# Modulation columns begun from GpSimd's queue in place of the queue that carries the weights

## The chip, the cores and the metric

The kernel runs on one core of one Trainium2 chip. The metric is the device time of one execution in microseconds (us), from the first to the last thing the core does for the program.

## The reference, cut to what matters

Two transformer blocks run one after the other on one sequence of 256 tokens with a width of 2048, all in float32. The first block takes six modulation vectors (shift, scale and gate, twice) from a conditioning vector `c`. The second block has no modulation.

```python
c_act = jax.nn.silu(c)
mod = c_act @ w_ada[l] + b_ada[l]                      # w_ada is 2048 x 12288
sh1, sc1, gt1, sh2, sc2, gt2 = jnp.split(mod, 6, axis=-1)
h = modulate(rms_norm(x, g_mix[l]), sh1, sc1)          # h * (1 + scale) + shift
z = h @ w_in[l]                                        # 2048 x 11344
...                                                    # two attentions, gates, two output products
x = x + gt1[:, None, :] * (merged @ w_out[l])
h = modulate(rms_norm(x, g_ffn[l]), sh2, sc2)
...                                                    # gated feed-forward
x = x + gt2[:, None, :] * y
```

So `sh1` and `sc1` are needed before the first large product can begin, `gt1` after the attentions, and the other three later. The second block is a gated linear attention and another feed-forward.

## The kernel before

Activations lie with features on the 128 partitions and the 256 tokens along a row, so a product needs weight tiles of 128x128 (or, for values, 128x512) in SBUF. Every weight tile group goes through `weights` (L89 to L102): a DMA on SyncE's queue brings 128x1024 float32 (512 KB) into a tile `raw`, ScalarE rounds it to `hi` (L96), VectorE subtracts to get the rest `lo` (L97), and TensorE multiplies `hi` and `lo` with the split activations. There are four buffers each of `raw`, `hi` and `lo`. Nearly all the rest of the kernel is this stream: 916 such groups in 2.7 ms. "Group n" below is the n-th of these, counted from 0, told by the n-th L97.

The modulation is not done on TensorE. The transposed `w_ada` is 96 blocks of 128x2048 float32 (1 MB each), one for each of 6 vectors times 16 feature tiles. `mod_fetch` (L200 to L207) takes the next block from a list `modq` and starts its DMA into a tile `col`, of which there are two buffers; `mod_reduce` (L209 to L215) multiplies it on VectorE by the broadcast `c_act` and sums along the row (L212), which gives one column of one vector. A third column can be fetched only when the first has been reduced.

In `mixer` the first 32 columns are interleaved with the first product, tile by tile: feature tile k of the activations (`h_mod`: L298 and L301 on VectorE, L300 on ScalarE) needs columns 2k and 2k+1. The first product is done in parts, `batch(b, k0, k1)`, for three groups of outputs b and for the feature tiles 0 to 1, 2 to 6 and 7 to 15, so that not all 16 tiles are needed at once; it takes 96 weight groups, and its products are L134, L135 and L136. The other 64 columns are spread by a credit (`self.rate`) over the weight groups that follow; fetches and weights are marked as of high priority.

The order of the instructions on each engine, and on each DMA queue, is not written by hand: the framework's scheduler sets it when the program is built, from the code's order, the priorities and its own estimate of durations. Once built it is fixed, and each engine and queue works in that order, waiting where something is not ready. Before the change every DMA of the program, columns and weights alike, is issued by SyncE's queue (SP); GpSimd (POOL) does nothing but four small memory settings at the start.

Of the kernel before, what the change touches and what calls it, by code (L numbers as in the profile page):

```python
# [19 lines left out]
KD = D // P  # L20
# [12 lines left out]
class Core:  # L33
# [166 lines left out]
    def mod_fetch(self, offset=120):  # L200
        if not self.modq:
            return
        ci, j = self.modq.popleft()
        with self.tc.high_priority(offset=offset):
            col = self.wp.tile([P, D], F32, name="col", tag="col", bufs=2)
            self.nc.sync.dma_start(col, self.ap["w_ada"][ci * KD + j])
        self.colq.append((ci, j, col))  # L207

    def mod_reduce(self):  # L209
# [930 lines left out]
```

## Time and profile before

| | |
|---|---|
| median of 2 runs | 2692.26 us (2686.73 to 2697.78) |
| the profiled execution's own time | 2694.12 us |
| its span, first to last instruction | 2692.3 us |
| mean granted TensorE clock | 0.997 of 2.4 GHz |
| TensorE (PE) matmul busy | 2661.8 us, 99% |
| VectorE (DVE) busy | 1875.0 us, 70% |
| ScalarE (ACT) busy | 1304.5 us, 48% |
| DMA | 585.64 MB, mean 218 GB/s |

The busy share of PE is an upper bound for the work done, since matmuls are pipelined and their ends are modelled. Shares over the whole span hide that the first 700 us, in which the columns are fetched, are unlike the rest: there the DMA engines and VectorE are much busier than later.

### The profile page before, as it was taken

How to read it: one execution, taken by the hardware profiler on the slowest of the kernel's cores; microseconds unless marked ns; L12 is line 12 of the kernel's file. 1: busy time of each engine (PE TensorE's matmuls, PEld its weight loads, DVE VectorE, ACT ScalarE, POOL GpSimd, SP SyncE). 2: the span in 40 equal slices, each digit the busy share in tenths (PEclk: the TensorE clock that was granted, in tenths of full speed). 3: DMA queues.
4: the chain of work that ended last, by engine and by line, in shares of the span. 5: the costliest groups of instructions: out<-in, count | busy, mean ns of one | idle time of the engine just before them, and what ended most of it. 6: DMA issues, size and time to landing. Idle time of an engine off the chain costs nothing.

```text
span 2692.3 us, 41008 instructions
## 1 busy us (share of the span) xinstructions
PE 2661.8 (99%) x15996; PEld 2352.1 (87%) x15996; DVE 1875.0 (70%) x2725; ACT 1304.5 (48%) x1927; POOL 0.2 (0%) x4
## 2 busy tenths in 40 slices
PE   7999999999999999999999999999999999999999
PEld 6999977889988888888888888888888888888888
DVE  7998897978877666666555677477666666665444
ACT  5433344544555444444444565465544444444333
POOL 0000000000000000000000000000000000000000
PEclk9999999999999999999999999999999999999999
DMA  9989889888655555555666545545555555556664
GB/s 347 344 331 330 326 296 308 318 303 316 233 172 188 188 188 189 190 189 187 188 188 188 178 142 150 171 148 188 181 180 188 188 188 188 188 188 184 201 198 144
DMA packets 153853, 585.64 MB, mean 218 GB/s; under 512 B 17047, under 2 KB 21879, under 8 KB 141369
## 3 DMA queue, kind: packets, MB, share of 16 engines
q1 hardware_dynamic: 153658, 583.02, 63.9%
q8 instruction: 125, 2.05, 0.3%
q14 instruction: 70, 0.57, 0.1%
HBM read 579.22 MB, written 3.67 MB: 217 GB/s over the span
## 4 chain that ended last, share of the span: by engine, by line
PE 88%; DMA 5%; DVE 4%; issue 2%; ACT 1%; SPq 0%; DVEq 0%; ACTq 0%
PE acc L107 47%; PE acc L110 24%; DMA col<-in_w_ada 4%; PE acc L136 3%; PE acc L135 3%; PE acc L134 2%; DVE lo L97 2%; PE misc L134 1%; PE misc L135 1%; PE misc L136 1%; PE acc L174 1%; PE acc L175 1%; PE acc L176 1%; DVE col L212 1%; PE misc L878 1%
## 5 line engine op out<-in xcount | busy, mean ns | idle before, releaser
L107 PE MATMUL acc<-slot,hi 128*128 128x512 f32 x5520 | 1847.5, 395 | 3.0 <-ACT hi L96 2.5
L97 DVE TENSOR_TENSOR lo<-raw,hi 128x1024 fp32r<-128x1024 f32 (+1 forms) x916 | 1101.3, 1205 | 695.9 <-ACT hi L96 694.9
L96 ACT CAST hi<-raw 128x1024 fp32r<-128x1024 f32 (+1 forms) x916 | 946.5, 1034 | 1222.3 <-issue 525.9
L110 PE MATMUL acc<-slot,lo 128*128 128x256 f32 x5520 | 1326.4, 281 | 0.8 <-DVE lo L97 0.8
L110 PEld LDWEIGHTS acc<-slot,lo 128*128 128x128 f32 x5520 | 1039.5, 188 | 116.9 <-DVE lo L97 1.1
L107 PEld LDWEIGHTS acc<-slot,hi 128*128 128x128 f32 x5520 | 948.0, 188 | 127.6 <-ACT hi L96 2.8
L212 DVE CUSTOM_DVE_ANT_0 col<-col,big,vecs 128x2048 f32<-128x2048 f32 x96 | 225.4, 2348 | 44.3 <-DMA col<-in_w_ada 44.1
L134 PE MATMUL acc<-slot,hi 128*128 128x256 f32 x656 | 182.7, 284 | 8.8 <-ACT hi L96 4.6
L135 PE MATMUL acc<-slot,hi 128*128 128x256 f32 x656 | 183.2, 283 | 0.2 <-DVE slot L301 0.2
L136 PE MATMUL acc<-slot,lo 128*128 128x256 f32 x656 | 177.8, 285 | 1.4 <-DVE lo L97 1.1
L134 PEld LDWEIGHTS acc<-slot,hi 128*128 128x128 f32 x656 | 124.0, 190 | 10.3 <-ACT hi L96 5.8
L135 PEld LDWEIGHTS acc<-slot,hi 128*128 128x128 f32 x656 | 124.8, 190 | 0.5 <-DVE slot L301 0.5
L136 PEld LDWEIGHTS acc<-slot,lo 128*128 128x128 f32 x656 | 121.4, 191 | 3.1 <-DVE lo L97 3.1
L134 PE MATMUL misc<-slot,hi 128*128 128x256 f32 x384 | 107.6, 283 | 0.6 <-ACT hi L96 0.6
L135 PE MATMUL misc<-slot,hi 128*128 128x256 f32 x384 | 107.2, 281 | 0.0
L136 PE MATMUL misc<-slot,lo 128*128 128x256 f32 x384 | 105.3, 282 | 1.8 <-DVE lo L97 1.8
L174 PE MATMUL acc<-hi,slot 128*128 128x512 f32 x256 | 103.2, 403 | 0.0
L175 PE MATMUL acc<-lo,slot 128*128 128x512 f32 x256 | 101.2, 395 | 0.0
L176 PE MATMUL acc<-hi,slot 128*128 128x512 f32 x256 | 101.1, 395 | 0.0
L185 ACT COPY t<-acc 128x256 f32<-128x256 f32 x234 | 85.7, 366 | 0.7 <-PE acc L110 0.7
L186 DVE TENSOR_TENSOR t<-acc,t 128x256 f32<-128x256 f32 x188 | 78.5, 418 | 0.0
L134 PEld LDWEIGHTS misc<-slot,hi 128*128 128x128 f32 x384 | 72.6, 189 | 1.3 <-ACT hi L96 1.2
(222 smaller groups left out, 1619.3 us busy)
## 6 DMA issues: line engine op xcount, KB each, us to landing
raw<-in_w_gu SPq DMA_DIRECT2D x344, 512.0 KB, 3.6
col<-in_w_ada SPq DMA_DIRECT2D x96, 1024.0 KB, 7.6
raw<-in_w_in_k SPq DMA_DIRECT2D x96, 512.0 KB, 6.7
raw<-in_w_down SPq DMA_DIRECT2D x80, 512.0 KB, 4.3
raw<-in_w_dn SPq DMA_DIRECT2D x80, 512.0 KB, 4.5
raw<-in_gla_b SPq DMA_DIRECT2D x66, 512.0 KB, 3.6
raw<-in_w_in_b SPq DMA_DIRECT2D x50, 512.0 KB, 5.7
raw<-in_w_in_a SPq DMA_DIRECT2D x32, 512.0 KB, 5.8
```

The lines of the kernel that those rows point to most:

```text
L96: self.mark = nc.scalar.copy(hi[:, :n], raw[:, :n])
L97: nc.vector.tensor_sub(lo[:, :n], raw[:, :n], hi[:, :n])
L107: self.nc.tensor.matmul(acc, hi, x, start=start, stop=stop, skip_group_check=True)
L110: self.nc.tensor.matmul(acc[:, 1], lo, x[:, 0], start=False, stop=stop, skip_group_check=True)
L134: nc.tensor.matmul(out, hi, x[:, 0], start=first, stop=False, **mm)
L135: nc.tensor.matmul(out, hi, x[:, 1], start=False, stop=False, **mm)
L136: nc.tensor.matmul(out, lo, x[:, 0], start=False, stop=last, **mm)
L174: nc.tensor.matmul(o, hs[k][:, 0, tt], hi[:, w], start=(k == 0), stop=False)
L175: nc.tensor.matmul(o, hs[k][:, 0, tt], lo[:, w], start=False, stop=False)
L176: nc.tensor.matmul(o, hs[k][:, 1, tt], hi[:, w], start=False, stop=(k == KD - 1))
L185: nc.scalar.copy(t, acc[:, 1])
L212: self.nc.vector.tensor_tensor_reduce(out=col, in0=col, in1=self.c_act, scale=1.0, scalar=self.vec["b_ada"][:, n:n + 1], op0=ALU.mult, op1 ...
```

## The change

One call moves from SyncE's queue to GpSimd's.

```diff
@@ mod_fetch
         ci, j = self.modq.popleft()
         with self.tc.high_priority(offset=offset):
             col = self.wp.tile([P, D], F32, name="col", tag="col", bufs=2)
-            self.nc.sync.dma_start(col, self.ap["w_ada"][ci * KD + j])
+            self.nc.gpsimd.dma_start(col, self.ap["w_ada"][ci * KD + j])
         self.colq.append((ci, j, col))
```

Since the scheduler builds the order anew, the change also moves instructions on all engines up to group 214 or so. Three places follow. A name such as `slot_203` is a buffer of activations (tile 0 of the modulated input), `mod_78` holds the scale vector, `mod_77` the shift vector, and `t_201` is an intermediate of `h_mod`.

SyncE's queue at the start, before: after the input tiles and the vectors come two columns and then weights and columns in turn.

```order
L517 DMA slot_94<-in_x 128x512
L519 DMA vecs<-in_vecs 128x356
L206 DMA col<-in_w_ada 128x2048 x2
L93 DMA raw<-in_w_in_k 128x1024 x2
L206 DMA col<-in_w_ada 128x2048 x2
L93 DMA raw<-in_w_in_k 128x1024 x2
L206 DMA col<-in_w_ada 128x2048
L93 DMA raw<-in_w_in_k 128x1024
```

The same place after: weights follow at once, and no column is on this queue.

```order
L517 DMA slot_94<-in_x 128x512
L519 DMA vecs<-in_vecs 128x356
L93 DMA raw<-in_w_in_k 128x1024 x6
L334 DMA cst<-in_cst 128x512
```

GpSimd after: the 96 columns stand alone behind the four settings, of which this is the last.

```order
L1128 MEMSET const-uint8-127 128x1
L1135 UNCONDITIONAL_BRANCH
L206 DMA col<-in_w_ada 128x2048 x96
L1135 UNCONDITIONAL_BRANCH
L1135 ISA
```

The 96 column transfers have moved and wait only for a free `col` buffer there.

ScalarE at the start, before: the square root of the norm (L243) stands right behind the squares of the input (L523).

```order
L523 ACTIVATE slot_115<-slot_94 128x512
L243 ACT_TABLE_LOAD
L243 ACTIVATE slot_159<-misc,eps 128x256
L96 CAST hi<-raw 128x1024 x2
L300 ACTIVATE slot_203<-t_201,mod_77 128x256
```

The same place after.

```order
L523 ACTIVATE slot_115<-slot_94 128x512
L96 CAST hi<-raw 128x1024 x3
L243 ACT_TABLE_LOAD
L243 ACTIVATE slot_159<-misc,eps 128x256
L96 CAST hi<-raw 128x1024
L300 ACTIVATE slot_203<-t_201,mod_77 128x256
```

Three weight casts now stand ahead of the square root.

VectorE between the first and the second column's reduction and the low half of activation tile 0 (L301), before.

```order
L212 ISA col,mod_78<-col,big,vecs 128x2048
L212 ISA mod_78 128x1
L244 RECIPROCAL slot_159<-slot_159 128x256
L555 SCALAR_TENSOR_TENSOR mod_78<-mod_78,vecs 128x1
L212 ISA col,mod_77<-col,big,vecs 128x2048
L212 ISA mod_77 128x1
L97 TENSOR_TENSOR lo<-raw,hi 128x1024
L298 SCALAR_TENSOR_TENSOR t_201<-slot_87,mod_78,slot_159 128x256
L97 TENSOR_TENSOR lo<-raw,hi 128x1024
L301 SCALAR_TENSOR_TENSOR slot_203<-t_201,mod_77,slot_203 128x256
```

The same place after; the first column's reduction and two L97 stand ahead of these rows.

```order
L555 SCALAR_TENSOR_TENSOR mod_78<-mod_78,vecs 128x1
L212 ISA col,mod_77<-col,big,vecs 128x2048
L212 ISA mod_77 128x1
L97 TENSOR_TENSOR lo<-raw,hi 128x1024 x2
L244 RECIPROCAL slot_159<-slot_159 128x256
L212 ISA col,mod_78<-col,big,vecs 128x2048
L212 ISA mod_78 128x1
L298 SCALAR_TENSOR_TENSOR t_201<-slot_87,mod_78,slot_159 128x256
L555 SCALAR_TENSOR_TENSOR mod_78<-mod_78,vecs 128x1
L212 ISA col,mod_77<-col,big,vecs 128x2048
L212 ISA mod_77 128x1
L301 SCALAR_TENSOR_TENSOR slot_203<-t_201,mod_77,slot_203 128x256
```

Two more column reductions and two more L97 now stand ahead of the first finished activation tile.

Counted along VectorE's row order: ahead of group 56 there are 32 column reductions before and after the change; from there up to group 168 there are 45 before and 64 after; behind group 168 there are 19 before and none after. Behind the first residual of `w_out` (L715, about group 214) nothing moves on any engine.

## Rows read from the trace of the kernel before

**Rows 1.** The page: span, PE's busy time, and GB/s in 40 slices.

```profile
span 2692.3 us, 41008 instructions
...
GB/s 347 344 331 330 326 296 308 318 303 316 233 172 188 188 188 189 190 189 187 188 188 188 178 142 150 171 148 188 181 180 188 188 188 188 188 188 184 201 198 144
```

**Rows 2.** Windows: stretch, length, PE, PEld, DVE, ACT, POOL busy, granted clock, DMA share, GB/s.

```profile
0.00:22.00 22.00, 13.14 (x40) 7.88 (x40) 14.16 (x21) 12.07 (x18) 0.20 (x4) 1.00 0.85 312
22.00:194.00 172.00, 163.34 (x1306) 159.00 (x1305) 162.40 (x208) 77.47 (x118) 0.00 (x0) 0.98 0.92 347
194.00:548.00 354.00, 349.42 (x2198) 309.55 (x2197) 297.21 (x441) 160.93 (x240) 0.00 (x0) 1.00 0.89 315
548.00:701.00 153.00, 149.41 (x1089) 141.90 (x1089) 131.39 (x177) 78.85 (x129) 0.00 (x0) 0.98 0.84 301
...
790.00:1500.00 710.00, 710.00 (x4077) 623.03 (x4076) 463.17 (x642) 351.03 (x506) 0.00 (x0) 1.00 0.58 188
```

**Rows 3.** VectorE's costliest lines, 0 to 194 us: busy us, mean ns | idle before.

```profile
L212 DVE CUSTOM_DVE_ANT_0 col<-col,big,vecs 128x2048 f32<-128x2048 f32 x32 | 75.1, 2346 | 4.7 <-DMA col<-in_w_ada 4.6
L97 DVE TENSOR_TENSOR lo<-raw,hi 128x1024 fp32r<-128x1024 f32 x56 | 67.6, 1219 | 3.6 <-ACT hi L96 3.3
```

**Rows 4.** The same view, 194 to 548 us.

```profile
L97 DVE TENSOR_TENSOR lo<-raw,hi 128x1024 fp32r<-128x1024 f32 x114 | 137.8, 1220 | 24.5 <-ACT hi L96 24.0
L212 DVE CUSTOM_DVE_ANT_0 col<-col,big,vecs 128x2048 f32<-128x2048 f32 x45 | 105.7, 2349 | 29.0 <-DMA col<-in_w_ada 28.9
```

**Rows 5.** The same view, 548 to 701 us.

```profile
L97 DVE TENSOR_TENSOR lo<-raw,hi 128x1024 fp32r<-128x1024 f32 x49 | 59.3, 1221 | 7.2 <-ACT hi L96 7.2
L212 DVE CUSTOM_DVE_ANT_0 col<-col,big,vecs 128x2048 f32<-128x2048 f32 x19 | 44.6, 2348 | 10.5 <-DMA col<-in_w_ada 10.5
```

**Rows 6.** The DMA queue's own waits on SP, 0 to 194 us: total, times, longest.

```profile
SPq L206 <- DVE mod L212: 70.7, 21, 7.4
...
SPq L206 <- DVE mod L555: 27.7, 8, 5.6
```

**Rows 7.** The DMA view, 0 to 194 us: GB/s in 40 slices of 4.85 us.

```profile
GB/s 162 342 419 362 319 331 354 318 360 403 360 347 371 423 389 394 335 378 408 258 193 344 367 367 293 409 351 313 257 305 377 412 356 188 345 394 342 354 423 289
```

**Rows 8.** Timeline of the start: start us, us, engine, line [idle before <- releaser].

```profile
11.04 1.28 ACT L243 ACT_TABLE_LOAD   x1
...
13.02 2.35 DVE L212 CUSTOM_DVE_ANT_0 col<-col,big,vecs 128x2048 f32<-128x2048 f32 x1 [1.28 <-DMA col<-in_w_ada]
...
13.91 0.47 ACT L243 ACTIVATE slot<-misc,eps 128x256 f32<-128x256 f32 x1 [1.59 <-PE misc L265]
...
15.30 1.75 DVE L244 RECIPROCAL slot<-slot 128x256 f32<-128x256 f32 x1
...
16.69 1.04 ACT L96 CAST hi<-raw 128x1024 fp32r<-128x1024 f32 x1 [2.31 <-DMA raw<-in_w_in_k]
...
20.38 0.48 DVE L298 SCALAR_TENSOR_TENSOR t<-slot,mod,slot 128x256 f32<-128x256 f32 x1
...
20.90 0.51 ACT L300 ACTIVATE slot<-t,mod 128x256 fp32r<-128x256 f32 x1 [1.93 <-DVE t L298]
21.46 0.78 PE L134 MATMUL acc<-slot,hi 128*128 128x256 f32 x4 [4.22 <-ACT slot L300]
...
22.45 0.58 PE L135 MATMUL acc<-slot,hi 128*128 128x256 f32 x1 [0.21 <-DVE slot L301]
```

**Rows 9.** The page's DMA issues: count, KB each, median us from issue to landing.

```profile
col<-in_w_ada SPq DMA_DIRECT2D x96, 1024.0 KB, 7.6
raw<-in_w_in_k SPq DMA_DIRECT2D x96, 512.0 KB, 6.7
```

**Rows 10.** The tile `col`: all its transfers.

```profile
DMA to landing us min/median/max: 4.7/7.6/10.0
```

## The prediction

> **What bounds the kernel now.** I read the page first: the span, and the slices of traffic, which fall from 347 to about 188 GB/s a quarter of the way in [rows 1]. The columns are fetched only in that first quarter, so I cut it into stretches by the trace: stretch A, 22 to 194 us, in which the 32 columns that the first product needs are reduced beside the first 56 weight groups [rows 2, 3]; B, 194 to 548 us, up to group 168, with 45 columns [rows 2, 4]; C, 548 to 701 us, with the last 19 [rows 2, 5]. Behind C nothing moves. The reader is to see in the windows that TensorE is the bound nearly everywhere: it is busy 163.34 of 172 us in A, 349.42 of 354 in B, 149.41 of 153 in C, and 710 of 710 in a long stretch with no columns [rows 2]. So its idle time is 8.7 us in A, 4.6 in B and 3.6 in C, together 16.9 us. A granted clock of 0.98 in A and C says that some 2% of the time (3.4 and 3.1 us) was lost at the lower of the two levels, 1.2 GHz [rows 2]. The start up to the first finished product tile, the L135 at 22.45 us [rows 8], is the only other idle time that the columns touch. **No change to the columns can win much over 30 us, about 1%.**
>
> The second thing to see is how near the bound VectorE and the DMA engines are in these stretches: VectorE is busy 162.4 of 172 us in A (94%), 297.2 of 354 in B (84%), 131.4 of 153 in C (86%), and the DMA share is 0.92, 0.89 and 0.84 [rows 2]. And the queue: in the first 194 us SP stood 70.7 + 27.7 us at a column's issue, waiting until VectorE had reduced an older column [rows 6], and all weights stood behind it. The traffic of that time swings between 188 and 423 GB/s [rows 7], which looks like a queue that runs dry now and then rather than one flat limit.
>
> **The change part by part.** *The issues.* 96 issues leave SP and stand on GpSimd, which has nothing else to do; no work is queued behind them there. SP loses the waits of [rows 6]; what it then waits for is a free `raw` buffer, set by VectorE's L97, as it does already between columns. That worth is contained in TensorE's idle time above, at most 8.7 us in A, and nothing in B and C beyond their 8.2 us.
>
> *A column's way.* The trace has no transfer from GpSimd. A buffer's cycle is its landing time plus one reduction of 2.35 us [rows 3], and there are two buffers, so a column costs (landing + 2.35)/2. By the order after the change, 64 columns stand in stretch B, one each 354/64 = 5.5 us: the landing may take up to 2 x 5.5 - 2.35 = 8.7 us before VectorE, which works in order, stands at L212 with all later L97 behind it. In A it is 172 us for about 32 columns, 5.4 us each, and 8.4 us. Today a column lands in 4.7 us at best, 7.6 in the middle, 10.0 at worst [rows 10], and in that time it is in one line with up to four weight transfers of 512 KB, which take 6.7 us to land themselves [rows 9]. On its own queue it skips that line, and pays for whatever GpSimd needs to begin it. The first can be worth 7.6 - 4.7 = 2.9 us, the second is unknown. I take 7.6 us as before, the middle row, hence no cost; the ends are 4.7 (no cost either) and 10.0 us, priced below as a rival.
>
> The Trainium skill, in "DMA: Bandwidth & Descriptors", section "Issuing engines are not separate DMA queues", says that transfers begun on several engines run on the same 16 DMA engines and that only the time to issue them is saved. No run here shows it yet; by it the landing would stay near 7.6 us, as I took it, and the line that a column skips would be worth nothing.
>
> *The start.* Now the first product begins at 21.46 us and goes on with L135 at 22.45 [rows 8]. After the change ScalarE does three casts ahead of the square root, so it waits for three weight groups. Ahead of the third lie the input (2.1 MB), the vectors (0.18 MB), two columns (2.1 MB) and three groups (1.6 MB): 6.0 MB, at the 347 GB/s of A 17 us, so it has landed at about 18 us. Then one cast (1.04), the table load (1.28) and the square root (0.47): 20.8 us. VectorE has the fourth group's L97 (its cast ends at 21.8, L97 takes 1.22, so 23.1), the reciprocal (1.75) and the third column's reduction (2.35): 27.2; then L298 (0.48) and ScalarE's L300 (0.51): the first L134 begins at 28.3 instead of 21.46. The second product needs L301, which stands behind the fourth column's reduction: that column is begun when the second has been reduced, at about 22 us, lands 7.6 us later, is reduced by 32 and L301 ends at 32.5. So L135 begins about 10 us later [rows 3, 8].
>
> *Stretch A.* In those 10 us weights pile up in the buffers, so part comes back. TensorE's need in A is 172 - 8.7 = 163.3 us; from 32.5 us that ends at 196, against 194 now, if it never waits again. VectorE has the same 32 reductions and 56 L97 in A. If half of the 8.7 us of waits stay, A ends at 200. Part of what TensorE lost at the low clock can come back, up to 3.4 us. **A: +4 us**, from -5 (the start hides as now, half the waits go) to +11.
>
> *Stretch B.* 19 columns come in from C. VectorE's busy time grows by 19 x 2.35 = 44.7 us, from 297.2 to 342 of 354 us, 97%. The traffic grows by 19 x 1.05 = 20 MB on 354 x 0.315 = 111.5 MB, to 131.5 MB, 371 GB/s over 354 us; slices of up to 423 exist [rows 7], a whole stretch above 347 does not [rows 2]. TensorE needs 349.4. Three engines at 97 to 99% with two and four buffers between them don't run without waits. If VectorE keeps all its waits of now, 28.9 us for columns and 24.0 for `hi` [rows 4], B takes 342 + 53 = 395 us, +41; if its waits all go, TensorE's 349.4 stay, -4.6. At 347 GB/s the traffic takes 379, +25. Waits for `hi` are TensorE's own slack and go first; columns on a line of their own should come more evenly. I take 3% of the stretch, nearer the lower end, since no engine is over 100% and the slices show bandwidth to spare: **B: +10 us**.
>
> *Stretch C.* Without its columns VectorE has 44.6 us less to do and the 10.5 us of waits for columns are gone [rows 5]. TensorE can win its idle 3.6 us and the clock's 3.1: at most 6.7. **C: -5 us**, from -7 to 0.
>
> The sum is +4 + 10 - 5 = **+9 us**, with ends of -17 and +52. The profiled execution took 2694.1 us, so it would take 2703; that is 1.8 us above the median of the runs, 2692.3, which gives **2701 us**.
>
> **The rivals.** *The queue set free.* What speaks for it: 98 us in which SP stood at a column's issue [rows 6], and the swings of the traffic [rows 7]. If weights always are ahead, the late start is hidden and B's load is smooth, all 16.9 us of idle time go: 2692 - 17 = 2675. Against it: the start's order is fixed, with three casts and four reductions ahead of the first tile.
>
> *GpSimd is slow to begin a column.* This one ends on the other side. A landing longer than about 8.5 us makes every column cost half of the excess, on VectorE, in A and in B: 96 x 0.5 = 48 us for each us of excess. With the longest landing of now, 10.0 us [rows 10], for all: 1.5 x 48 = 72, on top of the 9: 2773 us. It decides from 8.5 us, and makes the kernel over 2% slower from 8.5 + (54 - 9)/48 = 9.4 us. For it: the landing of 7.6 us leaves less than 1 us of room. Against it: 4.7 us shows that most of 7.6 is standing in line.
>
> The Trainium skill has a rule that would bring this about: "SBUF — State Buffer", section "SBUF: two separate sides", says that GpSimd writes the descriptors of its transfers itself, and is kept from it while VectorE runs an instruction in a mode that takes two SBUF ports, so that the transfer starts only when that instruction has ended. The trace does not bear out its condition so far: L97 takes 1219 ns for 1024 elements and L212 2346 for 2048 [rows 3], both about 1.15 ns per element, and none of the rows that I read is faster per element. If it held, a column would wait for the L97 or L212 that runs just then, 1.2 to 2.35 us, which is a landing of 8.8 to 10.0 us and a time of 2715 to 2773.
>
> That the change doesn't do what it says is no rival: the order shows all 96 issues on GpSimd's queue.
>
> **How the numbers follow.** Forecast (sums from 2684 to 2730): 0.6. The queue set free, 2675: 0.2. GpSimd slow, 2715 to 2773 and more: 0.2, of which 0.12 lie above 2746. A difference of 2%, 54 us, is about what a measurement of this kernel can tell from none. Faster by that: 2638 or less, which no case reaches, 0.02. Slower: 2746 or more, 0.13 with a bit for the upper end of B. The range takes in the queue set free and the upper end of B, and leaves the worst of GpSimd out: 2672 to 2748.
>
> **What would show it.** In the profile of the changed kernel the first L135 begins near 32 us instead of 22.45. VectorE's group 56 begins at 193 to 205 us, group 168 at 355 to 375 us after that, with 64 columns between them and VectorE busy over 95% of it, and groups 168 to 216 take 146 to 150 us with no column. The landing of the columns is the row that decides: at 7 to 8.5 us the forecast holds; over 9 us, with VectorE's waits for `col` above 100 us in all instead of 44 in the stretches above [rows 3 to 5], GpSimd is slow. If it falls to 5 or 6 us, and TensorE's idle time in A goes under 5 us, the queue set free is right. What would make the whole wrong is an effect behind 701 us, where nothing moves, or a clock that falls to its lower level for long because TensorE starts late and in pieces.

## The result and the profile after

After the change the median of 2 runs is 2735.77 us (2734.44 to 2737.10), against 2692.26 before: 1.0165 times the time before, 95% interval 1.014 to 1.019. It is a loss of 1.6%, inside the range, 35 us above the predicted 2701. The profiled execution took 2734.44 us, its span is 2732.6, so 40.3 us are to be explained. The page of after, its span, part 1 and the two queues of section 3 (packets, MB, share of 16 engines):

```profile
span 2732.6 us, 41100 instructions
...
PE 2670.2 (98%) x15996; PEld 2360.8 (86%) x15996; DVE 1878.3 (69%) x2725; ACT 1303.5 (48%) x1927; POOL 51.3 (2%) x100
...
q1 hardware_dynamic: 139834, 482.35, 52.9%
q0 software_dynamic: 13824, 100.67, 10.0%
```

The number of matmuls is that of before, 15996. They were busy 8.4 us longer (2670.2 against the 2661.8 of the table before), and TensorE stood idle 62.4 us (2732.6 - 2670.2) where it was 30.5 (2692.3 - 2661.8), 31.9 more. These are the 40.3 us: TensorE waited more, and was a little slower in between. Cut at the same weight groups (told by the n-th L97), the time went here: up to group 56 206.8 us instead of 194.2, +12.6; from there to group 168 386.2 instead of 353.8, +32.5; from 168 to 216 145.5 instead of 152.7, -7.2; all the rest +2.4 (differences taken before rounding). The windows of after, with the columns of [rows 2] and edges at about those groups and at groups 96 and 128:

```profile
34.00:207.00 173.00, 164.80 (x1317) 162.77 (x1318) 153.07 (x202) 75.87 (x116) 14.88 (x28) 0.96 0.88 329
207.00:340.00 133.00, 122.43 (x974) 120.99 (x974) 111.16 (x122) 43.70 (x42) 12.36 (x24) 0.95 0.90 342
340.00:441.00 101.00, 96.22 (x432) 74.33 (x431) 98.39 (x163) 42.49 (x55) 8.50 (x17) 0.98 0.87 328
441.00:593.00 152.00, 138.25 (x768) 118.72 (x767) 129.46 (x196) 74.11 (x143) 12.59 (x24) 0.97 0.91 326
593.00:739.00 146.00, 146.00 (x1091) 139.60 (x1090) 95.29 (x138) 77.64 (x127) 0.00 (x0) 1.00 0.57 190
...
828.00:1538.00 710.00, 710.00 (x4058) 619.76 (x4057) 462.19 (x641) 350.78 (x506) 0.00 (x0) 1.00 0.58 187
```

Rows two to four are stretch B: TensorE's idle time there is 29.1 us (386 - 356.90) where it was 4.6 [rows 2], and the granted clock is 0.95 to 0.98 where it was 1.00. In the row behind, without columns, both are gone at once, and in the long row TensorE is busy throughout, as it was before.

VectorE's costliest lines in B, 207 to 593 us, with the columns of [rows 4]:

```profile
L212 DVE CUSTOM_DVE_ANT_0 col<-col,big,vecs 128x2048 f32<-128x2048 f32 x64 | 150.2, 2347 | 32.7 <-DMA col<-in_w_ada 32.7
L97 DVE TENSOR_TENSOR lo<-raw,hi 128x1024 fp32r<-128x1024 f32 x112 | 135.4, 1218 | 5.0 <-ACT hi L96 4.7
```

There are 64 reductions instead of 45; the waits for columns stayed (32.7, before 28.9), and the waits for `hi` went from 24.0 to 4.7 [rows 4]. In A (0 to 207 us) the waits for columns rose from 4.6 [rows 3] to 16.7:

```profile
L212 DVE CUSTOM_DVE_ANT_0 col<-col,big,vecs 128x2048 f32<-128x2048 f32 x32 | 75.1, 2345 | 16.7 <-DMA col<-in_w_ada 16.7
```

The tile `col` of after, its issues and its transfers:

```profile
L206 POOL DMA_DIRECT2D col<-in_w_ada x96: 527/530/662, 1.3 to 578.0; - x96
...
DMA to landing us min/median/max: 4.9/6.7/11.3
```

The median landing is 6.7 us where it was 7.6 [rows 10]. What TensorE waited for in B (total, times, longest):

```profile
PE acc L110 <- DVE lo L97: 6.4, 3, 4.1
PE acc L134 <- DVE slot L584: 5.3, 2, 3.3
PE acc L174 <- DVE slot L584: 4.7, 1, 4.7
PE misc L453 <- ACT t L450: 3.8, 1, 3.8
PE acc L136 <- DVE lo L97: 2.4, 2, 2.2
```

Of these 22.6 us, 18.8 are a work of VectorE that came late. The start, in the timeline of after (columns as in [rows 8]):

```profile
15.50 2.35 DVE L212 CUSTOM_DVE_ANT_0 col<-col,big,vecs 128x2048 f32<-128x2048 f32 x1
...
20.62 0.47 ACT L243 ACTIVATE slot<-misc,eps 128x256 f32<-128x256 f32 x1
...
20.71 2.34 DVE L212 CUSTOM_DVE_ANT_0 col<-col,big,vecs 128x2048 f32<-128x2048 f32 x1
...
22.98 2.35 DVE L97 TENSOR_TENSOR lo<-raw,hi 128x1024 fp32r<-128x1024 f32 x2
...
25.26 1.74 DVE L244 RECIPROCAL slot<-slot 128x256 f32<-128x256 f32 x1
...
26.92 2.25 DVE L212 CUSTOM_DVE_ANT_0 col<-col,big,vecs 128x2048 f32<-128x2048 f32 x1
...
30.17 1.22 PE L134 MATMUL acc<-slot,hi 128*128 128x256 f32 x4 [6.44 <-ACT slot L300]
...
34.21 0.58 PE L135 MATMUL acc<-slot,hi 128*128 128x256 f32 x1 [1.96 <-DVE slot L301]
```

The first L134 and L135 stand 8.7 and 11.8 us later than in [rows 8].

### The profile page after: what moved, and what is told of

The parts are those of the page before. It is cut to its first block, busy times and chain, and to the rows that moved or that the text cites. A ratio compares the mean times of both kernels' runs of the same rounds, so it can differ in the third digit from the quotient of the medians.

```text
span 2732.6 us, 41100 instructions
## 1 busy us (share of the span) xinstructions
PE 2670.2 (98%) x15996; PEld 2360.8 (86%) x15996; DVE 1878.3 (69%) x2725; ACT 1303.5 (48%) x1927; POOL 51.3 (2%) x100
## 4 chain that ended last, share of the span: by engine, by line
PE 82%; issue 8%; DMA 5%; DVE 4%; POOL 1%; ACT 1%; SPq 0%; POOLq 0%; DVEq 0%; ACTq 0%
PE acc L107 46%; PE acc L110 24%; DMA raw<-in_w_in_k 2%; DVE lo L97 2%; PE acc L135 2%; PE acc L134 2%; PE acc L136 2%; PE acc L174 1%; PE acc L175 1%; PE acc L176 1%; DVE col L212 1%; PE misc L878 1%; DMA col<-in_w_ada 1%; DMA skew<-t 1%; POOL col L206 1%
## 5 line engine op out<-in xcount | busy, mean ns | idle before, releaser
L97 DVE TENSOR_TENSOR lo<-raw,hi 128x1024 fp32r<-128x1024 f32 (+1 forms) x916 | 1101.8, 1205 | 703.7 <-ACT hi L96 700.1
L212 DVE CUSTOM_DVE_ANT_0 col<-col,big,vecs 128x2048 f32<-128x2048 f32 x96 | 225.3, 2346 | 49.5 <-DMA col<-in_w_ada 49.4
L134 PE MATMUL acc<-slot,hi 128*128 128x256 f32 x656 | 189.9, 291 | 19.0 <-DVE slot L584 11.5
L135 PE MATMUL acc<-slot,hi 128*128 128x256 f32 x656 | 189.7, 289 | 2.0 <-DVE slot L301 2.0
L134 PEld LDWEIGHTS acc<-slot,hi 128*128 128x128 f32 x656 | 128.8, 197 | 20.5 <-issue 8.9
L135 PEld LDWEIGHTS acc<-slot,hi 128*128 128x128 f32 x656 | 129.3, 197 | 2.3 <-DVE slot L301 2.3
L134 PE MATMUL misc<-slot,hi 128*128 128x256 f32 x384 | 108.8, 285 | 2.3 <-DVE slot L584 2.0
L135 PE MATMUL misc<-slot,hi 128*128 128x256 f32 x384 | 107.9, 281 | 0.0
L134 PEld LDWEIGHTS misc<-slot,hi 128*128 128x128 f32 x384 | 72.8, 191 | 3.6 <-DVE slot L584 2.8
```

The costliest lines, as they stand in the source:

```text
L97: nc.vector.tensor_sub(lo[:, :n], raw[:, :n], hi[:, :n])
L134: nc.tensor.matmul(out, hi, x[:, 0], start=first, stop=False, **mm)
L135: nc.tensor.matmul(out, hi, x[:, 1], start=False, stop=False, **mm)
L212: self.nc.vector.tensor_tensor_reduce(out=col, in0=col, in1=self.c_act, scale=1.0, scalar=self.vec["b_ada"][:, n:n + 1], op0=ALU.mult, op1 ...
```

## The experiments

Two things changed at once, the queue and, since the program was ordered anew, the place of 64 columns on VectorE. The theory: it is the **order**, 64 reductions in B on a VectorE that has no slack there, each met before its data are there. The rivals: **GpSimd's queue** itself, and the **traffic** of 19 more columns in B. Each kernel was timed beside the kernel before. This table is worked out from the traces; the stretches are cut by the n-th L97, the columns are the L212 in B (pairs of half ones count once), and the waits are VectorE's for `col`, up to group 56 and in B. Each row is one trace. The kernel before, e4, e8 and e14 have the same order of reductions and L97 on VectorE up to group 56 and take 190.0 to 194.3 us there; the kernel after, e2, e3, e7 and e13 have another order in common and take 206.1 to 211.2. So differences of some 5 us between two traces say little.

| kernel | up to group 56 | B: 56 to 168 | 168 to 216 | columns in B | waits A / B | ratio, 95% interval |
|---|---|---|---|---|---|---|
| before | 194.2 | 353.8 | 152.7 | 45 | 4.6 / 28.9 | 1 |
| after | 206.8 | 386.2 | 145.5 | 64 | 16.7 / 32.7 | 1.0165, 1.014 to 1.019 |
| e1_late_gp | 197.0 | 390.5 | 145.5 | 63 | 6.1 / 38.6 | 1.0147, 1.0118 to 1.0176 |
| e2_first_gp | 206.1 | 356.5 | 148.7 | 48 | 17.2 / 33.7 | 1.0067, 1.0041 to 1.0094 |
| e3_gp_paced | 211.2 | 387.4 | 155.2 | 27 | 18.8 / 84.9 | 1.0254, 1.0219 to 1.029 |
| e4_sp_paced | 194.3 | 360.6 | 145.3 | 27 | 3.3 / 54.7 | 1.0019, 1.0006 to 1.0031 |
| e6_half_bytes | 197.0 | 382.6 | 145.1 | 63 | 13.4 / 30.2 | 1.0113, 1.0097 to 1.013 |
| e7_gp_late_reduce | 208.5 | 348.0 | 145.9 | 26 | 17.8 / 0 | 1.0045, 1.003 to 1.006 |
| e8_sp_late_reduce | 190.0 | 344.6 | 145.9 | 26 | 1.2 / 0 | 0.9974, 0.9961 to 0.9988 |
| e9_mix_late_reduce | 195.5 | 347.9 | 145.9 | 26 | 3.0 / 0 | 0.9988, 0.9979 to 0.9998 |
| e10_two_sp | 203.9 | 347.5 | 145.9 | 26 | 18.7 / 0 | 1.0004, 0.9993 to 1.0015 |
| e12_half_both | 212.3 | 381.0 | 145.7 | 48 | 39.4 / 47.7 | 1.0171, 1.0154 to 1.0188 |
| e13_packed_late | 207.6 | 383.2 | 145.5 | 62 | 16.9 / 32.6 | 1.0145, 1.0121 to 1.017 |
| e14_packed_late_sp | 191.8 | 412.2 | 140.4 | 64 | 2.4 / 5.9 | 1.0187, 1.0158 to 1.0216 |

### One part of the columns from GpSimd

The edit of e1 leaves the first 32 columns on SyncE's queue; e2 has `ci < 2` in its place, so that only the first 32 come from GpSimd.

```diff
-            self.nc.gpsimd.dma_start(col, self.ap["w_ada"][ci * KD + j])
+            q = self.nc.gpsimd if ci > 1 else self.nc.sync
+            q.dma_start(col, self.ap["w_ada"][ci * KD + j])
```

> The first 32 columns are begun from SyncE's queue as before, the other 64 from GpSimd's. VectorE's built order has 33 columns ahead of group 56 with the start as before, 63 between groups 56 and 168, none behind. Theory P (the rebuilt order packs 64 columns into the stretch of groups 56 to 168, where VectorE and TensorE are both near full): the stretch up to group 56 takes about 194 us as before, groups 56 to 168 about 386 as after the change, groups 168 to 216 about 146, total about 2718 us. Rival Q (a transfer begun from GpSimd is itself the loss: it lands late): two thirds of the loss, about 2721, with landings longer than 7.6 us. Rival S (the late start is the main loss and is carried on through the later stretches): near 2695.

> The other half: only the first 32 columns are begun from GpSimd's queue. The start is built as after the change, and 48 columns stand between groups 56 and 168, 16 behind. Theory P: group 56 at about 207 us as after the change, then groups 56 to 168 in 355 to 360 us, 168 to 216 in 150: total about 2708 us. Rival Q: one third of the loss, 2706 us, so this run alone does not part P from Q. Rival S: 2730 or more.

Measured: 2732.15 and 2712.35 us. The two losses come apart: with the later 64 columns from GpSimd, B takes 390.5 us with a start of 197.0; with the first 32, the start takes 206.1 and B only 356.5. In e1 the 63 columns stand packed in B as in after, in e2 they don't. The totals are 14 and 4 us above those of theory P, and the total of e1 alone would not part P from Q; but its landings, 7.0 us in the middle, are not the longer ones that Q asks for.

### Columns held back

In e3 each of the 64 later columns waits for the current weight group: GpSimd first copies one element of the `hi` of that group into the buffer. e4 does the same, with the transfer issued by SyncE.

```diff
@@ weights
+        self.last_hi = hi
@@ mod_fetch
+            if ci > 1:
+                self.nc.gpsimd.tensor_copy(col[:, 0:1], self.last_hi[:, 0:1].bitcast(F32))
             self.nc.gpsimd.dma_start(col, self.ap["w_ada"][ci * KD + j])
```

> All 96 columns are begun from GpSimd's queue, but each of the later 64 is held until the cast of the current weight group is done (GpSimd copies one element of it into the column's buffer, which the transfer then overwrites). VectorE's order then has 27 columns between groups 56 and 168 in place of 64, 14 up to 216 and 23 behind. Theory P: group 56 at about 207 us, groups 56 to 168 in 345 to 355, the next 48 in about 148, nothing lost behind: 2685 to 2703 us, a gain of 33 to 50 on the changed kernel. Rival Q: the queue is still GpSimd's for every column, so 2725 or more. Rival S: about 2730, since the start is unchanged.

> The same hold, with all columns on SyncE's queue as before the change: 27 columns between groups 56 and 168 in place of 45, 14 up to 216, 23 behind. The hold now stands on the queue of the weights. Theory P, if the order alone counts: 2692 less up to 8 us that the columns cost in those stretches, 2680 to 2692 us. If the wait at a column's issue keeps the weights behind it back (which is what a queue of its own is for): 2695 to 2720 us, and TensorE waits for casts. Rival Q says nothing of this run beyond 2692 or less.

Measured: 2759.69 and 2698.90 us. e3 missed its expectation. The hold took away the early start of the transfers, while VectorE's order still had L212 close behind, and VectorE waited 84.9 us in B for 27 columns; e7 below, with 26 columns and no hold, has no such wait. So it is not the number of columns alone that costs time; waits at the reduction do it too. e4 came out in the second of its ranges, 2695 to 2720 us.

The two edits differ in the queue alone, and VectorE's order in B is nearly the same, yet B takes 387.4 us in e3 and 360.6 in e4. The landings of the tile `col`, first in e3, then in e4:

```profile
DMA to landing us min/median/max: 4.9/7.7/10.1
```

```profile
DMA to landing us min/median/max: 4.7/6.5/10.1
```

So where a reduction stands close behind its transfer, the queue does make a difference, and here the separate one was the slower. The next kernels move the reduction, not the transfer.

### Half the bytes

e6 fetches half of each column and reduces that half twice, so that VectorE has about the work of after, with half the columns' traffic. Its output lacks half of the modulation's inputs.

```diff
-            col = self.wp.tile([P, D], F32, name="col", tag="col", bufs=2)
-            self.nc.gpsimd.dma_start(col, self.ap["w_ada"][ci * KD + j])
+            col = self.wp.tile([P, D // 2], F32, name="col", tag="col", bufs=2)
+            self.nc.gpsimd.dma_start(col, self.ap["w_ada"][ci * KD + j, :, :D // 2])
...
+        for h in (slice(0, D // 2), slice(D // 2, D)):
+          self.nc.vector.tensor_tensor_reduce(out=col, in0=col, in1=self.c_act[:, h], scale=1.0,
```

> As after the change, but a column transfer brings only half of its row (512 KB) and the half is reduced twice, against both halves of the activated vector, so half of the modulation's input is left out while VectorE's work stays (192 reductions of about 1.2 us). VectorE's order keeps the packing: 60 of 192 ahead of group 56, 184 ahead of 168, 192 ahead of 176. Theory P (VectorE too full from group 56 to 168): that stretch stays at 375 us or more, total 2720 or more. Theory W (columns that land later than the order allows for, and VectorE standing in front of them, 34 us in that stretch after the change): the waits fall under 10 us, the stretch to 350-358, total 2690 to 2708 us. Theory of traffic (S2: 371 GB/s wanted): the same as W, but the DMA share in the stretch would have to be at its limit after the change, and it was 0.87 to 0.91 as before it.

Measured: 2721.25 us. The window of its stretch B (columns of [rows 2]):

```profile
197.00:579.00 382.00, 358.18 (x2189) 315.80 (x2188) 344.79 (x605) 160.41 (x240) 32.94 (x62) 0.97 0.74 248
```

The DMA engines are at 0.74 and 248 GB/s, where after has 326 to 342; yet B takes 382.6 us and VectorE still waits 30.2 us for columns. **So the loss does not need the added traffic.** Since the waits did not fall under 10 us as theory W supposed, the run does not part VectorE's load from its waits.

### Reductions placed late

Here nothing is held back; the 64 later reductions are placed behind the L97 of the current group in VectorE's order, so that they are met when their columns have long landed. That also spreads them: 26 stand in B. e7 issues all columns from GpSimd, e8 all from SyncE, e9 the first 32 from SyncE and the others from GpSimd.

```diff
-            nc.vector.tensor_sub(lo[:, :n], raw[:, :n], hi[:, :n])
+            self.sub = nc.vector.tensor_sub(lo[:, :n], raw[:, :n], hi[:, :n])
...
+        with (self.tc.issue_after(self.sub.ins) if ci > 1 else ExitStack()):
             self.nc.vector.tensor_tensor_reduce(out=col, in0=col, in1=self.c_act, scale=1.0,
```

> All 96 transfers from GpSimd's queue, free to start as soon as a buffer is; only the reductions of the later 64 are placed in VectorE's order behind the L97 of the weight group at which the code asks for them: 26 between groups 56 and 168, 14 up to 216, 24 behind. A column then has landed long before its reduction. Theories P and W (order and waits on VectorE, not the queue): VectorE's waits for these columns under 10 us in all, groups 56 to 168 in 345 to 352, the total 2692 + 12 for the start - 4 - 5 = 2695 us (2688 to 2703). Rival Q (a transfer begun from GpSimd costs time by itself): 2720 or more, with waits for columns left.

> The same late reductions with all transfers on SyncE's queue, as before the change. If order alone counts: start as before, 56 to 168 in 345 to 352, total 2692 - 9 = 2683 us (2678 to 2690). If a column's issue that waits for its buffer holds the weights back on the shared queue: 2695 or more, with TensorE or ScalarE waiting for weights behind group 56; that would be the place where a queue of its own is worth something.

> First 32 columns from SyncE as before, the later 64 from GpSimd with late reductions. If the start on GpSimd costs about 12 us and the queue nothing: the kernel with late reductions all on GpSimd less 12, 2683 us (2678 to 2690), a little faster than the kernel before. Rival Q: 2710 or more.

Measured: 2700.80, 2683.96 and 2687.73 us. The windows of B in e7 and e8:

```profile
208.00:557.00 349.00, 344.93 (x2179) 305.82 (x2178) 257.91 (x405) 161.15 (x240) 14.35 (x27) 1.00 0.74 260
```

```profile
190.00:535.00 345.00, 345.00 (x2188) 306.94 (x2187) 257.48 (x402) 161.85 (x240) 0.00 (x0) 1.00 0.77 268
```

And VectorE's two lines in that window of e7 (columns of [rows 4]):

```profile
L97 DVE TENSOR_TENSOR lo<-raw,hi 128x1024 fp32r<-128x1024 f32 x113 | 137.9, 1223 | 73.8 <-ACT hi L96 73.7
L213 DVE CUSTOM_DVE_ANT_0 col<-col,big,vecs 128x2048 f32<-128x2048 f32 x27 | 63.3, 2345 | 0.0
```

With the columns on the very queue that after uses, B takes 348 us instead of 386, no column is waited for in it, and VectorE's waits for `hi`, 73.7 us, show that it has slack again. The three choices of queue give 348.0, 344.6 and 347.9, and the three totals lie in the ranges of the theory of order: **with the reductions placed late the loss in B is gone, and the queue changes nearly nothing there.** e8, which keeps the old queue, is the fastest of all, 0.26% under the kernel before (interval 0.12 to 0.39%). Its windows show a TensorE that never stands in B, which makes 345 us the floor of that stretch. What is left of e7's loss lies up to group 56: 208.5 us, with 17.8 us of waits for columns.

### The first two columns from SyncE

On top of e7, in which the columns' order at the start is that of after:

```diff
+            q = self.nc.gpsimd if offset else self.nc.sync
+            q.dma_start(col, self.ap["w_ada"][ci * KD + j])
```

> As the kernel with all columns from GpSimd and late reductions (2701 us, group 56 at 208.5 us), but the first two columns are begun from SyncE's queue, behind the input; the other 94 from GpSimd. The square root then stands ahead of all casts again, and the first finished activation tile needs two reductions and two L97. If the late start is the built order of the first tile together with the input sharing the engines with two columns: first L135 near 22.5 us, group 56 at 193 to 198, total about 2688 us. If the first stretch is longer for another reason (the 30 columns that still come from GpSimd): group 56 stays near 207 and the total near 2700.

Measured: 2694.03 us, group 56 at 203.9 instead of 208.5, between the two expectations. The start itself did come back, to within half a microsecond of [rows 8]:

```profile
21.87 1.22 PE L134 MATMUL acc<-slot,hi 128*128 128x256 f32 x4 [2.73 <-ACT slot L302]
22.89 0.56 PE L135 MATMUL acc<-slot,hi 128*128 128x256 f32 x1
```

Yet only 4.6 of the 14.3 us that e7 loses up to group 56 to the kernel before went with it, about as much as two traces of one order differ by, and 203.9 is still 9.6 us above the longest of the four traces with the order of before. The late start is thus the smaller part of that loss. The rest stays, and VectorE still waits 18.7 us for columns; e9, with all 32 on SyncE's queue, has 195.5 and 3.0. Two causes remain that no run parts: VectorE's order up to group 56, which in e10 is not that of before, and GpSimd's issue, which up to group 56 ends 0.8 to 1.0 us after the reduction that frees the buffer (trace of after), where SyncE's ends after 0.4 (before).

### VectorE's load or its waits

e12 fetches half of each column and reduces it once: half the work on VectorE too (and half of the modulation's inputs left out). It is e6 with `for h in (slice(0, D // 2),):`.

> As the kernel with half the bytes of each column, but each half is reduced once instead of twice: VectorE's work for the columns is halved too, again with half of the modulation's input left out. The order packs the columns even closer: 48 between groups 56 and 112, none behind. Theory P (VectorE full): VectorE's busy time between groups 56 and 168 falls from 350 to about 255 us, and the stretch from 382 to 345-355; total about 2685 us. If it is the packing as such, whatever VectorE's load: 375 or more, total 2715 or more.

Measured: 2738.02 us. The columns moved forward once more: 35 stand between groups 56 and 96. VectorE there (212 to 354 us):

```profile
L97 DVE TENSOR_TENSOR lo<-raw,hi 128x1024 fp32r<-128x1024 f32 x41 | 49.3, 1219 | 0.9 <-ACT hi L96 0.9
L213 DVE CUSTOM_DVE_ANT_0 col<-col,big,vecs 128x1024 f32<-128x1024 f32 x35 | 44.8, 1283 | 39.8 <-DMA col<-in_w_ada 39.8
```

Its busy time is 101.0 of 141.7 us, far from full, and the waits of 39.8 fill the rest (140.8 together). That VectorE's load alone makes the loss is refuted; load and waits have to be added.

e13 and e14 were to show the load without the waits: the late reductions of e7 and e8, at a credit at which all columns stand in B as in after.

```diff
-        self.rate = 0.25
+        self.rate = 0.61
```

(Likewise for the rates 0.2, 0.15 or 0.38, and 0.33 of the code behind.)

> All columns from GpSimd with late reductions, but the code asks for them as densely as the changed kernel's order has them: 62 between groups 56 and 168 (64 there), 2 behind. VectorE's load in the stretch is that of the changed kernel, about 335 us; only the places of the reductions are even and no longer those that the scheduler chose. Theory W (a stretch takes the longer of TensorE's need and of VectorE's busy time plus its waits for columns): if the waits fall from 34 to under 12 us, groups 56 to 168 take 348 to 358 us, total about 2708. Theory P (VectorE's load alone): 380 or more, total 2733 or more. If the waits stay at 30 or more in spite of the even places, a column each 5.5 us is more than two buffers carry, and the run says nothing of load alone.

> The same dense, late reductions with all transfers on SyncE's queue: 64 columns between groups 56 and 168. Theory W: start as before the change, group 56 at 190 to 195; the stretch depends on the waits for columns as above: 348 to 360 if under 15 us, total 2685 to 2700; the shared queue adds waits of the weights behind a column's issue, so it may be 10 us worse than the same on GpSimd. If GpSimd's queue is what makes columns late: clearly fewer waits here than with GpSimd.

Measured: 2732.27 and 2743.09 us. e13 does not separate them: at a column every 6 us its waits are 32.6 us again. In e14 VectorE waits for columns only 5.9 us in B, and B is the longest of all, 412.2 us. First TensorE's, then the waits of SyncE's queue, both in B of e14 (192 to 604 us):

```profile
PE acc L107 <- ACT hi L96: 11.6, 5, 6.5
PE acc L134 <- ACT hi L96: 7.5, 3, 3.6
```

```profile
SPq L206 <- DVE mod L213: 204.2, 52, 6.6
SPq L93 <- DVE lo L97: 35.0, 29, 3.0
```

TensorE waits for casts, that is for weights: the queue stood 204.2 us at a column's issue, with the weights behind it. In after the same view (SyncE's waits, 207 to 593 us) has no L206:

```profile
SPq L93 <- DVE lo L97: 197.0, 70, 7.2
```

At this density the queue of one's own does what the change is about: e13 needs 383.2 us for B with 62 columns, e14 412.2 with 64. In the whole time 11 us of that are left, since e13 also has the late start.

One sign that e14's expectation names for a late GpSimd queue did come, clearly fewer waits for columns than in e13: 5.9 us against 32.6. The landings are 5.5 us in the middle in e14 and 7.4 in e13. With few, late columns it is the other way round, 6.4 us in e8 and 5.2 in e7, so a transfer from GpSimd is not late by itself. That it is later where the weights run beside it, and not held behind its issue, fits both pairs and was not tested alone.

## Why the prediction held, and where its sizes were off

**The number** lies in the range, but not where the forecast put it. 2735.77 us is above 2730, where the forecast's own sums end, and inside 2715 to 2773, the band of the rival of a slow GpSimd, whose mechanism the traces don't show. It was held by the room that the range left for the upper end of B, and in that the hit is partly luck. Three of the stated signs failed as well: group 168 came 386.2 us after group 56 and not 355 to 375, VectorE was busy 88% of that (339.01 of 386 us) and not over 95%, and the landing of 6.7 us, called the row that decides, lies between the 7 to 8.5 of the forecast and the 5 or 6 of the queue set free.

**The start** came late as forecast, and 2 us later still. L134 was forecast at 28.3 us and came at 30.17, L135 at 32.5 and came at 34.21. What held it is VectorE's row of work, which has no pause from 20.71 us to the end of the third column's reduction at 29.17; the prediction had the second column reduced by about 22 us, which came at 23.05, and counted one of the two L97 behind it. The late square root held nothing up: it ended at 21.09, and the reciprocal that reads it came at 25.26, behind those two L97.

**Stretch A** had the right sign and the wrong size: +4 forecast, +12.6 measured, a little over the upper end of +11. The step that failed is "if half of the 8.7 us of waits stay". TensorE's idle time behind the late start is 8.2 us (173 - 164.80), so nearly all stayed, and the clock, which was to give back up to 3.4 us, fell from 0.98 to 0.96. VectorE's waits for columns rose from 4.6 to 16.7 us. By e10 a late start that partly comes back, the prediction's picture of A, is the smaller part of the loss; why the columns are met too early is not settled.

**Stretch B** is the term that was mis-sized: +10 forecast, +32.5 measured, inside the ends of -4.6 and +41. VectorE's busy time was forecast at 342 us and is 339.01; that the waits for `hi` go first was right. The step that failed is "3% of the stretch, nearer the lower end, since no engine is over 100%". An average of 97% over 354 us hid where the columns stand. By the trace, TensorE alone needs 111, 100 and 133.5 us for groups 56 to 96, 96 to 128 and 128 to 168 (e8, in which it never stands there). VectorE's busy time and its waits at the reductions in after are 110.7 + 18.9 = 129.6 us of 132.5; 99.5 + 1.4 = 100.9 of 102.1; and 129.0 + 12.4 = 141.4 of 151.6, where 7.4 us more are a wait for a skewed copy. VectorE had become the bound in every part of B: its busy time alone was 97 to 100% of TensorE's need, and the waits for columns came on top. Before, the same sum in the first part was 87.9 + 12.8 = 100.7 of 113.1 us: there the waits were free. The sum does not tell all: in e3 it is 108.3, 101.8 and 132.0 us in the three parts, hardly above TensorE's need, and B took 387.4; its longest single wait for a column is 7.7 us, in after 5.8. The prediction had these waits in its upper end, 28.9 us if those for columns all stay, and chose against it because columns on a line of their own "should come more evenly". They did not: the median landing is shorter, but the longest went from 10.0 to 11.3 us, and the waits for columns in B from 28.9 to 32.7.

**The landing** was right to a microsecond (7.6 assumed, 6.7 found), and still did not decide. The room of 8.7 us was worked out from a column every 5.5 us; between groups 56 and 96 there are 23 columns in 111 us of TensorE's need, one every 4.8, which leaves 2 x 4.8 - 2.35 = 7.3 us, and 11 of these 23 landings are longer.

**Stretch C** was right: -5 forecast, -7.2 measured, at the lower end of -7. Behind it +2.4 us.

**The rival of a slow GpSimd** is not seen: the shortest landing in after is 4.9 us, the median 6.7, and e7 and e9 have medians of 5.2 and 5.1. By the single packets in the traces, a column's first packet starts 0.71 us after the issue in B of e7 (GpSimd) and 0.64 in B of e8 (SyncE), in the middle. The rule of the Trainium skill in "SBUF — State Buffer", section "SBUF: two separate sides", by which an instruction of VectorE that takes two SBUF ports keeps GpSimd from writing a transfer's descriptors, would have shown in landings of 8.8 to 10.0 us in the middle; L97 and L212 run at their old durations (1218 and 2347 ns), so no row shows its condition met, and no run here tells more. **The queue set free** is not seen either in after; SyncE's waits only changed their name, to L93 behind L97. What the Trainium skill says in "DMA: Bandwidth & Descriptors", section "Issuing engines are not separate DMA queues", agrees with e7 to e9, where the queue changes B by 3.4 us at most. It does not cover e13 and e14: there the issue that waits for a buffer holds back other transfers, and a second queue is worth 29 us in B. In e3 and e4 the second queue costs 27 us in B.

**The clock** took its share, as feared in one sentence: 0.991 over the span instead of 0.997, and 8.4 us of longer busy time for the same matmuls.

What stays open: how much of B's loss would remain if 64 columns stood there with no waits at all, since e13 has its waits back and e14 is held by its weights; and what makes the waits for columns in A.

## What to carry to other kernels

Where a scheduler rebuilds the order, count the moved work in the smallest stretches that have different limits, and add an engine's waits to its busy time there: once that sum passes what the bounding engine needs, further waits add to the time, as in every part of B here. A sum below that need is no promise, as e3 shows. Place a step that consumes a prefetched buffer well behind its transfer in its engine's order; here that was worth more (0.3% under the kernel before, with the old queue) than a queue of its own. A second queue paid where an issue that waits for a buffer would have held back transfers that others need (B of e13 against e14), and cost where each transfer was met at once (B of e3 against e4).

## What the runs showed of the hardware

Issues from GpSimd took 527 to 530 ns each, against 327 to 328 for most of SyncE's (e8). Which queue lands a column sooner depends on the rest: in the middle 5.2 us from GpSimd and 6.4 from SyncE in e7 and e8, but 7.7 and 6.5 in e3 and e4, and 7.4 and 5.5 in e13 and e14.

The longer pauses of TensorE are paid twice. In the first 600 us of after the granted clock fell nine times, each time in or behind a pause, and four times in those of before. The timeline of after, TensorE alone, behind a pause of 4.66 us:

```profile
345.64 0.72 PE L174 MATMUL acc<-hi,slot 128*128 128x512 f32 x1 [4.66 <-DVE slot L584]
346.16 0.63 PE L175 MATMUL acc<-lo,slot 128*128 128x512 f32 x1
...
348.79 0.55 PE L174 MATMUL acc<-hi,slot 128*128 128x512 f32 x1
349.18 0.39 PE L175 MATMUL acc<-lo,slot 128*128 128x512 f32 x1
```

The same matmul takes 0.63 us and then 0.39: behind the pause the granted clock was at the lower of its two levels, 1.2 GHz, before it was back at 2.4. So the stretches of after in which TensorE waits show 0.95 to 0.98 in their windows, and those without waits 1.00.
